# Two lanes of experts, merged third by third, in the mixture-of-experts stage of a two-block kernel

## The chip, the core and the metric

The kernel runs on one core of a Trainium2 chip. The metric is the device time of one execution in microseconds (us); smaller is better. The median of three runs of the kernel before is 2901.98 us (2898.53 to 2902.94).

## What is computed

A first block of two hybrid layers, a second mixer, and then the part that the change touches: a mixture of experts over 512 tokens of width 1024, with 32 experts, 4 chosen for each token, all in float32.

```python
top_vals, top_idx = lax.top_k(logits, TOP_K)
top_gates = jax.nn.softmax(top_vals, axis=-1)
...
gate = xb @ w_gate[e] + b_gate[e]
up = xb @ w_up[e] + b_up[e]
gate = jnp.minimum(gate, SWIGLU_LIMIT)
up = jnp.clip(up, -SWIGLU_LIMIT, SWIGLU_LIMIT)
glu = gate * jax.nn.sigmoid(SWIGLU_ALPHA * gate)
return (glu * (up + 1.0)) @ w_down[e] + b_down[e]
```

Each expert has three 1024 x 1024 float32 matrices, 12 MB, and all 32 are read whatever the routing is: 384 loads of 1 MB.

## The kernel before

The first 1,600 us or so (the dense part) are the two layers and the mixer; the change only moves some of their small constants to another pool. Then `route` and `rank` sort the experts by how many tokens they got. Rank 31 in that order is always expert 0, which is begun before the sorting is done.

**Kinds of expert.** A plan gives each rank its blocks of tokens. In the plan that runs here (`FEW`, line 1928) ranks 0 and 1 have two blocks of 128, ranks 2 to 4 one of 128 and one of 64, ranks 5 to 10 and 31 one of 128, and ranks 11 to 30 one block of at most 64. The text calls them B (0, 1), L (2 to 4), s (5 to 10 and 31) and T (11 to 30). If some expert has more tokens than its blocks hold, another branch runs with the plan `SLOTS`.

**Split and whole weights.** For B, L and s each half of a loaded 1 MB chunk (128 x 1024) is split in two: ACT rounds it to the high part (line 244) and DVE subtracts to get the low part (line 245). The four slots of `ws` hold split halves, and PE multiplies three times (high by high, high by low, low by high). T experts are "twins": PE reads their raw weights as they were loaded (`gu<-raw,xf`, `dn<-raw,hf` in the profile), with no split.

**Thirds.** An expert is three thirds of 4 chunks, 8 halves: gate and up projection for the first half of the features (written here as `r.0`), the same for the second half (`r.1`), and the down projection (`r.2`). Between them `turn` transposes the activations; `find` and `fetch` look up the block's tokens, gather their rows with an indirect DMA, and transpose them.

**Closing.** After a third, its results leave PSUM through ACT and DVE: for a T gate-and-up third ACT's Silu on line 1674 and then DVE; for a T down third two scalings on ACT, line 1747, and a scatter-add by an indirect DMA from POOL; for the others lines 1693, 1766 and their like. `later` collects these instructions, and `catch_up` issues them a few at a time during the third that follows.

**The order.** One list by hand gives the order of ranks: 11, 0, 12, 13, 5, 14, 2, 15, 16, 6, ... (second part of `FEW`). The loop in `ranked` goes gate-and-up 0 of the current rank, down of the rank before, gate-and-up 1 of the current one. So for rank 0 the thirds run 0.0, 11.2, 0.1, 12.0, 0.2, 12.1, 13.0, 12.2, 13.1, 5.0, 13.2, 5.1, ... A third of split weights always follows a T third, 34 times in all after 31.1.

**What sets the order of instructions.** Only PE's are in the order in which the code names them:

```python
with self.tc.manual_schedule(engines={mybir.EngineType.PE}):
```

The instructions of ACT, DVE, POOL and SP are put in order when the program is built, by when the builder reckons that each one's inputs are there. On the chip each engine then runs them in that fixed order.

**Loads.** SP issues all weight loads into a ring of nine 1 MB buffers (`raws`, `NRAW`). A load waits until the chunk nine before it was used: split by ACT and DVE, or, if whole, multiplied by PE. `split_ahead` names loads and splits up to 4 split halves ahead, and up to 12 halves in all.

Of the kernel before, what the change touches and what calls it, by code (L numbers as in the profile page):

```python
# [17 lines left out]
P = 128  # L18
# [26 lines left out]
def _constants():  # L45
# [24 lines left out]
    c[:, C_FEW:C_FEW + NE] = _np.array([sum(s) for s in FEW[0]])[None, :]  # L70
# [135 lines left out]
class _Kernel:  # L206
# [160 lines left out]
    def setup(self):  # L367
# [5 lines left out]
        vecs = self.const.tile([P, NV], F32, name="vecs")  # L373
# [5 lines left out]
        self.ones = self.const.tile([P, P], F32, name="ones")  # L379
        nc.vector.memset(self.ones, 1.0)  # L380
        self.onesr = self.const.tile([P, P], F32R, name="onesr")
        nc.vector.memset(self.onesr.bitcast(F32), 1.0)
        self.identb = self.const.tile([P, P], BF16, name="identb")
        nc.vector.tensor_copy(self.identb, self.ident)
        self.maskb = self.const.tile([P, P], BF16, name="maskb")
# [14 lines left out]
        self.mod = [self.const.tile([P, 48], F32, name="mod%d" % l) for l in range(2)]  # L400

    def position_tables(self):
# [27 lines left out]
        self.sp = self.const.tile([P, 16], F32, name="sp")  # L430
# [6 lines left out]
        self.spr = self.const.tile([P, 16], F32, name="spr")  # L437
        nc.vector.reciprocal(self.spr, self.sp)
        nc.vector.tensor_scalar(self.spr, self.spr, 200.0, 4.0, op0=OP.mult, op1=OP.max)
        self.spn = self.const.tile([P, 16], F32, name="spn")  # L440
        nc.vector.tensor_scalar(self.spn, self.sp, -1.0, None, op0=OP.mult)
        self.hb = self.const.tile([P, 2, 16], F32, name="hb")
# [120 lines left out]
    def slot(self):  # L563
        self.nu += 1
        return self.us[:, self.nu % 4]
# [765 lines left out]
    def rank(self, tp):  # L1331
# [4 lines left out]
        bank = lambda: self.ps2.tile([P, T], F32, tag="gu", name="gu", bufs=4)  # L1336
# [35 lines left out]
        for j in range(4):  # L1372
# [4 lines left out]
                   mo.tile([P, 4, NE], F32, tag="bs", name="gr", bufs=4))  # L1377

        cnt = mo.tile([NE, P], F32R, tag="bs", name="cnt", bufs=4)
# [25 lines left out]
    def down_bias(self, j):  # L1405

        nc = self.nc
        y = self.mo.tile([P, D], F32, tag="yy", name="yb", bufs=3)
        for n in range(2):
            p, w = self.ps2.tile([P, T], F32, tag="dn", name="dn", bufs=2), slice(n * T, (n + 1) * T)  # L1410
# [39 lines left out]
    def overflow(self):  # L1450
# [5 lines left out]
        with tc.For_i(0, n, 1) as it:  # L1456
# [25 lines left out]
            bs = mo.tile([96, P], BF16, tag="bs", name="bs", bufs=4)  # L1482
# [29 lines left out]
    def find(self, b, gate):  # L1512
# [12 lines left out]
        b["idx"] = self.small.tile([P, 1], I32, tag="idx", name="idx", bufs=6)  # L1525
# [7 lines left out]
        b["g"] = self.small.tile([P, 1], F32, tag="gsl", name="gsl", bufs=6)  # L1533
# [47 lines left out]
    def queue(self, srcs):  # L1581

        self.todo += [(s, i, w) for s, w in srcs for i in range(2)]

    def split_ahead(self, n):


        nc = self.nc
        while self.todo and len(self.halves) < 2 * NRAW - 6:
            src, i, whole = self.todo[0]  # L1590
            if not whole and sum(lo is not None for _, lo in self.halves) >= n:
                break
            self.todo.pop(0)
            if i == 0:
                self.raw = self.raws[self.nload % NRAW]
                self.nload += 1
                nc.sync.dma_start(self.raw, src)
            raw = self.raw[:, 1024 * i:1024 * i + 1024]
            if whole:
                self.halves.append((raw, None))  # L1600
                continue
            w = self.ws[self.nsplit % (AHEAD + 1)]
            self.nsplit += 1
            self.split(raw, w[:, 0], w[:, 1])
            self.halves.append((w[:, 0], w[:, 1]))

    def weights(self):
        self.split_ahead(AHEAD + 1)
        self.catch_up(CU + len(self.later) // CV)
        return self.halves.pop(0)  # L1610
# [19 lines left out]
    def gate_up(self, n, bsel, blocks, among=()):  # L1630

        nc, mo = self.nc, self.mo
        among = list(among)
        if blocks[0]["twin"]:
            return self.gate_up_twin(n, bsel, blocks[0], among)
        ps = [[self.ps2.tile([P, T], F32, tag="gu", name="gu", bufs=4) for _ in range(2)] for _ in blocks]
        for c in range(4):
            for i in range(2):
# [9 lines left out]
                self.step(among, k)  # L1648
# [4 lines left out]
    def step(self, among, k):  # L1653
        while among and (among[0][0] <= k or k == KD - 1):
            among.pop(0)[1]()

    def gate_up_twin(self, n, bsel, b, among):


        p = self.ps2.tile([P, T], F32, tag="gu", name="gu", bufs=4)  # L1660
        for k in range(KD):
# [8 lines left out]
            self.step(among, k)  # L1670
# [45 lines left out]
    def down(self, n, blocks):  # L1716
        nc, mo = self.nc, self.mo
        ps = [self.ps2.tile([P, T], F32, tag="dn", name="dn", bufs=2) for _ in blocks]
        for c in range(2):
            for i in range(2):  # L1720
                wt = self.weights()
                for z in range(2):
                    k, w = 2 * i + z, slice(z * T, (z + 1) * T)
                    for p, b in zip(ps, blocks):
                        self.product(p, b, b["h%d" % c], k, [x[:, w] for x in wt], c == 0 and k == 0, c == 1 and k == 3)
        for p, b in zip(ps, blocks):
# [6 lines left out]
    def down_twin(self, b):  # L1733

        nc = self.nc
        p = self.ps2.tile([P, T], F32, tag="dn", name="dn", bufs=2)
        rows = (p[0:64], p[64:P])
        for c in range(2):
            w = [self.weights()[0] for _ in range(4)]
            for k in range(4):  # L1740
                x = slice(k % 2 * T, k % 2 * T + T)
                for z in range(2):
                    self.mm(rows[z], b["h%d" % c][:, k], w[2 * z + k // 2][:, x], c == 0 and k == 0, c == 1 and k == 3)
        b["y"] = y = self.mo.tile([P, D], F32, tag="yy", name="yy", bufs=3)
# [31 lines left out]
    def first_weights(self):  # L1776
        self.todo, self.halves, self.later, self.nsplit, self.nload = [], [], [], 0, 0
# [6 lines left out]
    def experts(self):  # L1784
# [4 lines left out]
        self.us, self.nu, self.nx = mo.tile([P, 4, T], F32, name="u"), 0, 0  # L1789
        self.xts = self.pair(mo, [P, 2, D], "xt")  # L1790
        self.xgs, self.ng = mo.tile([P, XG, D], F32, name="xg"), 0
        nc.gpsimd.memset(self.xgs, 0.0)
        b = self.block(self.pos[:, :, 0], P)
# [13 lines left out]
        state = lambda: (list(self.todo), list(self.halves), self.nsplit, self.nload, self.raw, self.nu, self.nx, self.ng)  # L1807
        kept, first = state(), dict(b)
        with self.tc.If(many == 0) as fits:  # L1809
            self.ranked(cur, *FEW)  # L1810
        with fits.Else():
            self.todo, self.halves, self.nsplit, self.nload, self.raw, self.nu, self.nx, self.ng = kept
            b.clear()
            b.update(first)
            self.ranked(cur, SLOTS, RANKS, True)
            self.overflow()

    def selector(self, r):
        bs = self.mo.tile([96, P], BF16, tag="bs", name="bs", bufs=4)
# [3 lines left out]
    def ranked(self, cur, slots, ranks, more=False):  # L1823

        nc, mo = self.nc, self.mo
        SP = mybir.EngineType.SP
        order = list(self.chosen)

        def blocks_of(r):
            return [self.block(p[:, :, r], n, slots[r] == (64,)) for p, n in zip((self.posS, self.posB), slots[r])]  # L1830

        def start(r, blocks):
            for b in blocks:
                self.find(b, lambda j: self.gates[:, j, r])
            e = nc.values_load(self.order[0:1, r:r + 1], engines=(SP,), min_val=0, max_val=NE - 1)
            order.append(self.chunks(e, slots[r] == (64,)))
            return self.selector(r), blocks

        def down(blocks):
            if blocks[0]["twin"]:  # L1840
                return self.down_twin(blocks[0])
            for n in range(2):
                self.down(n, blocks)


        def tiles(blocks, us):
            c = sum(0.9 if b["twin"] else 1.4 if b["n"] == P else 0.95 for b in blocks)
            return max(0, min(KD - 1, int(us / c)))

        def fetches(cur, nxt, us):  # L1850

            k = tiles(cur, us)
            return [(k + i, f) for i, f in enumerate([f for b in nxt for f in self.fetch(b)])]

        with self.tc.manual_schedule(engines={mybir.EngineType.PE}):
            nxt = start(ranks[0], blocks_of(ranks[0]))
            self.queue(order[1][0])
            self.gate_up(1, *cur, [(0, lambda: self.turn(cur[1], 0))])
            for f in self.fetch(nxt[1][0]):
                f()  # L1860
            for i in range(1, NE):
                prev, cur = cur, nxt
                self.queue(order[i - 1][2:] + order[i][1])
                among = [(tiles(cur[1], 4), lambda: self.turn(prev[1], 1))]
                if i + 1 < NE:
                    r = ranks[i]
                    found, got = blocks_of(r), []
                    among.insert(0, (tiles(cur[1], 2), lambda: got.append(start(r, found))))
                self.gate_up(0, *cur, among)
                if i + 1 < NE:  # L1870
                    nxt = got[0]
                    self.queue(order[i + 1][0])
                else:
                    self.queue(order[i][2:])
                if i == 1 and more:
                    self.overflow_list()
                down(prev[1])
                self.gate_up(1, *cur, [(0, lambda: self.turn(cur[1], 0))] +
                             (fetches(cur[1], nxt[1], 4) if i + 1 < NE else []))
            self.catch_up()  # L1880
            self.turn(cur[1], 1)
            down(cur[1])
            self.catch_up()
# [31 lines left out]
XG = 2  # L1915
# [64 lines left out]
```

## Time and profile before

| | us |
|---|---|
| median of 3 runs | 2901.98 |
| the profiled execution | 2903.9 |
| its span | 2902.0 |
| PE busy, whole span | 2728.3 (94%) |
| experts, from 31.0's first matmul to 30.2's last, about 1683 to 2875 | 1192 |

A profile is one execution. Its span is the time from its first to its last instruction, and 1.9 us lie around it. "Idle before, releaser" says how long an engine stood still before an instruction and what ended that wait. The granted clock of PE is 1.00 at its upper level (2.4 GHz) and 0.50 at its lower one (1.2 GHz); between them a stretch was at both.

### The profile page before, as it was taken

What the parts mean: (1) busy time and instruction counts of PE and PEld (TensorE: products, weight loads), DVE (VectorE), ACT (ScalarE), POOL (GpSimd) and SP (SyncE); (2) the same over time, 40 slices, a digit from 0 to 9 for tenths busy, and PEclk for the clock granted to TensorE, in tenths of its full rate; (3) what the DMA queues carried; (4) which work ended last, traced back from release to release, by engine and by line L of the source; (5) the groups of instructions that cost most, each with busy time, mean ns of one, the idle gap of its engine ahead of it and who ended that gap; (6) DMA issues with size and microseconds to landing.
All of it is one profiled execution on the core that took longest, in us unless ns stands there. A gap on an engine that the chain in (4) does not pass through costs nothing. (4 is left out here: it accounts for less than half of the span.)

```text
span 2902.0 us, 33795 instructions
## 1 busy us (share of the span) xinstructions
PE 2728.3 (94%) x12644; PEld 1927.0 (66%) x12644; DVE 1583.9 (55%) x2601; ACT 1124.0 (39%) x1655; POOL 217.6 (7%) x207
## 2 busy tenths in 40 slices
PE   7989999999999999999999889989999999999985
PEld 5677888888877788888777656546446446446452
DVE  7877676365686663333488664354444345335353
ACT  3644442222554442222344344344333334334342
POOL 0100000000000000000011010110100210110100
PEclk8999999999999999999999989999999999999998
DMA  6332446365221233333221586997997998998995
GB/s 230 122 113 93 160 160 223 118 213 165 94 69 59 65 99 102 95 96 99 89 73 62 190 317 266 338 409 295 384 399 304 346 407 354 366 409 320 371 386 214
DMA packets 126078, 629.42 MB, mean 217 GB/s; under 512 B 15632, under 2 KB 19088, under 8 KB 76752
## 3 DMA queue, kind: packets, MB, share of 16 engines
q1 hardware_dynamic: 111744, 593.94, 54.2%
q0 software_dynamic: 8288, 23.86, 3.8%
q10 hardware_dynamic: 5872, 9.36, 0.9%
q8 instruction: 101, 1.65, 0.2%
q14 instruction: 73, 0.60, 0.1%
HBM read 607.31 MB, written 24.38 MB: 218 GB/s over the span
## 5 line engine op out<-in xcount | busy, mean ns | idle before, releaser
L236 PE MATMUL acc<-hh,whi 128*128 128x512 f32 (+1 forms) x1496 | 574.7, 388 | 13.9 <-ACT hh L506 6.2
L236 PE MATMUL acc<-hh,wlo 128*128 128x512 f32 (+1 forms) x1496 | 576.5, 387 | 5.2 <-DVE wlo L245 5.1
L236 PE MATMUL acc<-hl,whi 128*128 128x512 f32 (+1 forms) x1496 | 574.2, 385 | 0.7 <-DVE hl L507 0.7
L245 DVE TENSOR_TENSOR wlo<-raw,whi 128x1024 fp32r<-128x1024 f32 (+2 forms) x253 | 305.6, 1210 | 268.4 <-ACT whi L244 266.7
L245 DVE TENSOR_TENSOR w<-raw,w 128x1024 fp32r<-128x1024 f32 x288 | 341.1, 1219 | 188.7 <-ACT w L244 186.9
L244 ACT ACTIVATE whi<-raw 128x1024 fp32r<-128x1024 f32 (+2 forms) x253 | 258.9, 1024 | 471.5 <-PE acc L236 417.9
L236 PE MATMUL gu<-w,xth 128*128 128x512 f32 x896 | 313.9, 429 | 44.1 <-ACT w L244 29.0
L244 ACT ACTIVATE w<-raw 128x1024 fp32r<-128x1024 f32 x288 | 293.0, 1051 | 111.6 <-PE gu L236 67.5
L236 PEld LDWEIGHTS acc<-hh,whi 128*128 128x128 f32 x1496 | 282.1, 190 | 78.5 <-ACT hh L506 9.0
L236 PEld LDWEIGHTS acc<-hh,wlo 128*128 128x128 f32 x1496 | 283.3, 189 | 62.4 <-DVE wlo L245 6.3
L236 PEld LDWEIGHTS acc<-hl,whi 128*128 128x128 f32 x1496 | 283.6, 190 | 56.4 <-issue 3.1
L236 PE MATMUL gu<-raw,xf 128*64 128x512 f32 x1280 | 305.8, 601 | 0.7 <-ACT xf L1549 0.7
L236 PEld LDWEIGHTS gu<-w,xth 128*128 128x128 f32 x896 | 173.3, 198 | 100.4 <-ACT w L244 42.7
L236 PE MATMUL gu<-w,xtl 128*128 128x512 f32 x448 | 183.4, 409 | 0.0
L236 PEld LDWEIGHTS gu<-raw,xf 128*64 128x64 f32 x1280 | 82.3, 136 | 128.8 <-issue 122.7
L236 PE MATMUL dn<-w,hTh 128*128 128x512 f32 x448 | 148.0, 407 | 20.5 <-ACT w L244 11.5
L236 PE MATMUL dn<-raw,hf 128*64 128x512 f32 x640 | 143.0, 600 | 0.0
L236 PEld LDWEIGHTS dn<-w,hTh 128*128 128x128 f32 x448 | 85.2, 192 | 56.3 <-ACT w L244 17.6
L1675 DVE TENSOR_SCALAR u<-gu 64x512 f32<-64x512 f32 x40 | 27.3, 682 | 159.7 <-ACT g L1674 159.7
L828 DVE TENSOR_TENSOR t<-t,acc 128x512 f32<-128x512 f32 x44 | 30.3, 688 | 143.6 <-PE acc L236 134.6
L236 PEld LDWEIGHTS dn<-raw,hf 128*64 128x64 f32 x640 | 45.3, 138 | 89.8 <-issue 89.7
L1753 POOL DMA_INDIRECT accd<-yy,idx x37 | 58.3, 1576 | 590.8 <-ACT yy L1766 264.3
(685 smaller groups left out, 3914.8 us busy)
## 6 DMA issues: line engine op xcount, KB each, us to landing
raw<-in_wgu SPq DMA_DIRECT2D x256, 1024.0 KB, 12.5
raw<-in_wd SPq DMA_DIRECT2D x128, 1024.0 KB, 12.3
raw<-in_ws SPq DMA_DIRECT2D x220, 512.0 KB, 3.5
adaw<-in_wada SPq DMA_DIRECT2D x72, 512.0 KB, 4.8
raw<-in_wada SPq DMA_DIRECT2D x24, 512.0 KB, 5.0
raw<-in_ws SPq DMA_DIRECT2D x24, 384.0 KB, 3.0
xy<-in_xT SPq DMA_DIRECT2D x16, 256.0 KB, 4.6
raw<-in_ws SPq DMA_DIRECT2D x9, 256.0 KB
```

The source lines that it names most:

```text
L236: self.nc.tensor.matmul(ps, l, r, start=first, stop=last)
L244: self.nc.scalar.activation(hi, src, AF.Copy)
L245: self.nc.vector.tensor_sub(lo, src, hi.bitcast(F32))
L828: nc.vector.tensor_mul(u, s, ps[1])
L1675: lambda: nc.vector.tensor_scalar(u, p[0:64], 8.0, -6.0, op0=OP.min, op1=OP.max),
L1753: self.nc.gpsimd.indirect_dma_start(out=self.acc_d[:, :], out_offset=bass.IndirectOffsetOnAxis(ap=b["idx"][0:m, 0:1], axis=0), in_=b["y"][ ...
```

## The change

Two lanes are made. One holds rank 31 and then s, B and L experts by turns (31, 5, 0, 6, 1, 7, 2, 8, 3, 9, 4, 10), the other the T experts 11 to 30. `_merged` interleaves their thirds so that each lane's sum of |PE time of a half minus load time of a half| grows alike, by the constants 1.4, 0.95 and 0.9 us of work and 1.3 us of load; a split third is only put behind a T third. The order that comes out begins

```
31.0 31.1 T11.0 31.2 T11.1 5.0 T12.0 5.1 T11.2 5.2 T12.1 0.0 T13.0 0.1 T12.2 T13.1 T14.0 T13.2
0.2 T14.1 T15.0 T14.2 T15.1 6.0 T16.0 6.1 T15.2 6.2 T16.1 1.0 T17.0 1.1 T16.2 T17.1 T18.0 T17.2 1.2
```

and for rank 2 it has `2.0 T 2.1 T T T 2.2`, for ranks 3 and 4 `x.0 T x.1 T T x.2`. `find`, `fetch` and `turn` become jobs with due times on a clock that adds up the constants. Loads are named as soon as the ring has room; splits are named when they are among the next 4 halves, whole ones counted. The PSUM banks of both projections become one pool of six. There is a third gather buffer, for T alone, and `oh` has two buffers, `bs` five, `idx` and `gsl` eight.

```diff
-        vecs = self.const.tile([P, NV], F32, name="vecs")
+        vecs = self.main.tile([P, NV], F32, name="vecs")
...
     def slot(self):
-        self.nu += 1
-        return self.us[:, self.nu % 4]
+        return self.mo.tile([P, T], F32, tag="u", name="u", bufs=4)
...
-        b = {"n": n, "twin": twin, "oh": self.mo.tile([P, 4, P], BF16, tag="oh", name="oh", bufs=3)}
+        b = {"n": n, "twin": twin, "oh": self.mo.tile([P, 4, P], BF16, tag="oh", name="oh", bufs=2)}
...
-        self.ng += 1
-        b["x"] = x = self.xgs[:, self.ng % XG]
+        if not b["twin"]:
+            self.ng += 1
+        b["x"] = x = self.xgs[:, 2 if b["twin"] else self.ng % 2]
...
-        self.todo += [(s, i, w) for s, w in srcs for i in range(2)]
+        self.todo += srcs
+
+    def load_ahead(self):
+
+        while self.todo and self.nload < (self.freed + NRAW if len(self.raws) == NRAW else len(self.raws)):
+            src, whole = self.todo.pop(0)
+            raw = self.raws[self.nload % NRAW]
+            self.nc.sync.dma_start(raw, src)
+            self.loaded += [(raw[:, 1024 * i:1024 * i + 1024], whole, self.nload) for i in range(2)]
+            self.left.append(2)
+            self.nload += 1
...
     def split_ahead(self, n):
...
-        nc = self.nc
-        while self.todo and len(self.halves) < 2 * NRAW - 6:
-            src, i, whole = self.todo[0]
-            if not whole and sum(lo is not None for _, lo in self.halves) >= n:
-                break
...
+        self.load_ahead()
+        while self.loaded and len(self.halves) < n:
+            raw, whole, c = self.loaded.pop(0)
             if whole:
-                self.halves.append((raw, None))
+                self.halves.append((raw, None, c))
                 continue
             w = self.ws[self.nsplit % (AHEAD + 1)]
             self.nsplit += 1
             self.split(raw, w[:, 0], w[:, 1])
-            self.halves.append((w[:, 0], w[:, 1]))
+            self.free(c)
+            self.load_ahead()
+            self.halves.append((w[:, 0], w[:, 1], c))
...
-        ps = [[self.ps2.tile([P, T], F32, tag="gu", name="gu", bufs=4) for _ in range(2)] for _ in blocks]
+        ps = [[self.ps2.tile([P, T], F32, tag="gu", name="gu", bufs=6) for _ in range(2)] for _ in blocks]
...
-                self.step(among, k)
+                self.tick(sum(HALF_US[b["n"], False] for b in blocks))
...
+        def ask(x):
+
+            r = x["r"]
+            x["blocks"] = [self.block(p[:, :, r], n, x["whole"]) for p, n in zip((self.posS, self.posB), plan[r])]
+
+            def find():
+                for b in x["blocks"]:
+                    self.find(b, lambda j: self.gates[:, j, r])
+                x["bs"] = self.selector(r)
+                x["come"] = self.clock + 14.0
+                if x["whole"] or x.get("room"):
+                    fetch(x)
+
+            self.jobs.append((self.clock + 1.5, ("find", r), find))
...
         with self.tc.manual_schedule(engines={mybir.EngineType.PE}):
-            nxt = start(ranks[0], blocks_of(ranks[0]))
-            self.queue(order[1][0])
-            self.gate_up(1, *cur, [(0, lambda: self.turn(cur[1], 0))])
...
+            ask(xs[lanes[1][0]])
+            ask(first["next"])
+            turned(first, 0)
+            for i, (x, p) in enumerate(steps):
+                queue(i)
+                if p == 0:
+                    self.finish_jobs(("find", x["r"]))
...
+                    self.finish_jobs(("fetch", x["r"]))
+                    if x["next"]:
+                        ask(x["next"])
+                if p < 2:
+                    self.gate_up(p, x["bs"], x["blocks"])
+                    turned(x, p)
...
+                self.catch_up()
+                self.finish_jobs(("turn", x["r"]))
+                if x["whole"]:
+                    self.down_twin(x["blocks"][0])
...
+HALF_US = {(128, False): 1.4, (64, False): 0.95, (64, True): 0.9}
+LOAD_US = 1.3
...
+def _merged(plan, lanes):
...
+    one = [(r, p) for r in lanes[0] for p in range(3)]
+    q = lanes[1]
+    two = [(q[0], 0), (q[0], 1)]
+    for a, b in zip(q, q[1:]):
+        two += [(b, 0), (a, 2), (b, 1)]
+    two.append((q[-1], 2))
+    over = lambda r: abs(sum(HALF_US[n, plan[r] == (64,)] for n in plan[r]) - LOAD_US)
+    all1, all2 = sum(over(r) for r, _ in one[2:]), sum(over(r) for r, _ in two)
+    out, one = one[:2], one[2:]
+    d1 = d2 = 0.0
+    while one or two:
+        if one and (not two or d1 / all1 <= 1.1 * d2 / all2 and out[-1][0] in q):
+            out.append(one.pop(0))
+            d1 += over(out[-1][0])
+        else:
+            out.append(two.pop(0))
+            d2 += over(out[-1][0])
+    return out
```

## Rows read from the trace of the kernel before

**Rows 1.** The page, part 1 (PE) and part 2 (granted clock in 40 slices).

```profile
PE 2728.3 (94%) x12644; PEld 1927.0 (66%) x12644; DVE 1583.9 (55%) x2601; ACT 1124.0 (39%) x1655; POOL 217.6 (7%) x207
...
PEclk8999999999999999999999989999999999999998
```

**Rows 2.** Busy time by stretch: length; PE, PEld, DVE, ACT, POOL; clock, DMA share, GB/s.

```profile
1683.00:2875.00 1192.00, 1118.96 (x5105) 627.51 (x5103) 523.29 (x659) 455.08 (x614) 125.70 (x105) 0.97 0.91 353
...
2300.00:2400.00 100.00, 91.91 (x428) 47.17 (x427) 44.60 (x60) 37.62 (x52) 16.48 (x11) 0.97 1.02 410
```

**Rows 3.** Waits from 1690 to 2880: us in total, times, longest.

```profile
PE gu L236 <- ACT w L244: 29.0, 17, 1.9
...
PE gu L236 <- DVE w L245: 15.1, 17, 1.1
...
PE dn L236 <- ACT w L244: 11.5, 7, 1.6
...
PE dn L236 <- DVE w L245: 7.9, 7, 1.1
ACT w L244 <- DMA raw<-in_wgu: 5.9, 2, 3.2
```

**Rows 4.** Groups of instructions, 1690 to 2880: busy, mean ns, idle before.

```profile
L236 PE MATMUL gu<-w,xth 128*128 128x512 f32 x885 | 309.4, 429 | 44.1 <-ACT w L244 29.0 <-DVE w L245 15.1
...
L244 ACT ACTIVATE w<-raw 128x1024 fp32r<-128x1024 f32 x283 | 287.8, 1051 | 108.0 <-PE gu L236 67.5 <-PE dn L236 32.2 <-DMA raw<-in_wgu 5.9
...
L236 PE MATMUL dn<-w,hTh 128*128 128x512 f32 x448 | 148.0, 407 | 20.5 <-ACT w L244 11.5 <-DVE w L245 7.9 <-ACT yy L1766 0.9
```

**Rows 5.** Timeline of ACT behind the T third 16.2: start, length, what.

```profile
2087.67 0.68 ACT L1747 ACTIVATE yy<-dn,gsl 64x512 f32<-64x512 f32 x1 [7.14 <-PE dn L236]
2088.25 1.99 ACT L244 ACTIVATE w<-raw 128x1024 fp32r<-128x1024 f32 x2
2090.27 0.69 ACT L1747 ACTIVATE yy<-dn,gsl 64x512 f32<-64x512 f32 x1
2090.98 2.01 ACT L244 ACTIVATE w<-raw 128x1024 fp32r<-128x1024 f32 x2
```

**Rows 6.** Timeline of PE in the same place.

```profile
2080.51 7.09 PE L236 MATMUL dn<-raw,hf 128*64 128x512 f32 x32
2089.35 0.50 PE L236 MATMUL gu<-w,xth 128*128 128x512 f32 x1 [1.75 <-ACT w L244]
2090.61 0.51 PE L236 MATMUL gu<-w,xth 128*128 128x512 f32 x1 [0.76 <-DVE w L245]
```

**Rows 7.** Timeline of ACT before 0.1 and before 2.1.

```profile
1778.87 3.89 ACT L244 ACTIVATE w<-raw 128x1024 fp32r<-128x1024 f32 x4
1786.11 1.40 ACT L1747 ACTIVATE yy<-dn,gsl 64x512 f32<-64x512 f32 x2 [3.35 <-PE dn L236]
...
1975.05 1.99 ACT L244 ACTIVATE w<-raw 128x1024 fp32r<-128x1024 f32 x2
1980.37 0.69 ACT L1747 ACTIVATE yy<-dn,gsl 64x512 f32<-64x512 f32 x1 [3.34 <-PE dn L236]
1980.96 2.00 ACT L244 ACTIVATE w<-raw 128x1024 fp32r<-128x1024 f32 x2
```

**Rows 8.** By stretch: 2.0, 2.1, 6.1, 1.0, 1.1, four T thirds.

```profile
1947.50:1973.10 25.60, 22.84 (x94) 15.13 (x92) 13.22 (x16) 9.81 (x13) 1.86 (x1) 0.93 0.89 348
1979.90:2002.10 22.20, 22.20 (x102) 15.43 (x100) 8.89 (x9) 9.72 (x13) 2.21 (x2) 1.00 0.93 365
...
2087.20:2104.90 17.70, 15.19 (x64) 10.96 (x62) 10.28 (x9) 10.92 (x13) 2.09 (x2) 0.90 1.02 411
...
2163.70:2194.20 30.50, 27.77 (x114) 20.32 (x112) 14.26 (x18) 10.78 (x15) 1.36 (x1) 0.89 0.90 373
2201.00:2226.10 25.10, 25.10 (x118) 19.37 (x116) 9.96 (x10) 11.30 (x14) 1.71 (x2) 1.00 0.84 321
...
2257.40:2289.70 32.30, 32.30 (x167) 11.38 (x166) 4.56 (x9) 5.98 (x12) 6.29 (x6) 1.00 0.94 332
```

**Rows 9.** Timeline of PE at the first matmul behind the branch.

```profile
1700.54 0.28 PE L236 MATMUL tps<-gates,oh 128*128 128x6 bf16 x4 [3.27 <-DVE oh L1503]
```

**Rows 10.** Timeline of POOL: the clearing of the gather buffers, and what follows.

```profile
1649.71 1.81 POOL L1792 MEMSET xg<- 128x2048 f32 x1 [60.17 <-PE acc L236]
1670.05 0.40 POOL L1317 COPY G<-G 128x256 f32<-128x256 f32 x1 [18.54 <-DVE G L1316]
```

More of the change, by code (lines that the diff above doesn't have):

```diff
@@ L1609, in weights @@
         self.catch_up(CU + len(self.later) // CV)
-        return self.halves.pop(0)
+        hi, lo, c = self.halves.pop(0)
+        self.used.append(c if lo is None else None)
+        if len(self.used) > 4:
+            c = self.used.pop(0)
+            if c is not None:
+                self.free(c)
+        return hi, lo
+    STATE = "todo", "loaded", "halves", "left", "used", "nsplit", "nload", "freed", "nx", "ng"
     def catch_up(self, n=None):
@@ L1651, in gate_up, with gate_up_twin @@
             self.later += self.gated(p, b["n"], b["u%d" % n])
[L1653 to L1660, printed above, removed]
+    def gate_up_twin(self, n, bsel, b):
+        p = self.ps2.tile([P, T], F32, tag="gu", name="gu", bufs=6)
         for k in range(KD):
@@ L1725, in down @@
                         self.product(p, b, b["h%d" % c], k, [x[:, w] for x in wt], c == 0 and k == 0, c == 1 and k == 3)
+                self.tick(sum(HALF_US[b["n"], False] for b in blocks))
         for p, b in zip(ps, blocks):
@@ L1776, in first_weights @@
     def first_weights(self):
-        self.todo, self.halves, self.later, self.nsplit, self.nload = [], [], [], 0, 0
+        self.todo, self.loaded, self.halves, self.left, self.used, self.later = [], [], [], [], [], []
+        self.nsplit, self.nload, self.freed = 0, 0, 0
         self.raws, self.ws = [], []
@@ L1806, in experts @@
         many = nc.values_load(self.many[0:1, 0:1], min_val=0, max_val=1)
-        state = lambda: (list(self.todo), list(self.halves), self.nsplit, self.nload, self.raw, self.nu, self.nx, self.ng)
-        kept, first = state(), dict(b)
+        copied = lambda: {k: list(v) if isinstance(v, list) else v for k, v in ((k, getattr(self, k)) for k in self.STATE)}
+        kept, first = copied(), dict(b)
         with self.tc.If(many == 0) as fits:
-            self.ranked(cur, *FEW)
+            self.ranked(cur, FEW)
@@ L1820, in selector, with ranked @@
         self.nc.gpsimd.tensor_copy(bs, self.perm[:, r:r + 1].bitcast(F32).to_broadcast([96, P]))
         return bs
-    def ranked(self, cur, slots, ranks, more=False):
-        nc, mo = self.nc, self.mo
+    def ranked(self, cur, plan):
         SP = mybir.EngineType.SP
[L1827 to L1853, printed above, removed]
-        with self.tc.manual_schedule(engines={mybir.EngineType.PE}):
-            nxt = start(ranks[0], blocks_of(ranks[0]))
-            self.queue(order[1][0])
-            self.gate_up(1, *cur, [(0, lambda: self.turn(cur[1], 0))])
[L1859 to L1872, printed above, removed]
-                else:
[L1874 to L1879, printed above, removed]
@@ new lines, in ranked @@
+        lanes = _lanes(plan)
+        xs = {r: {"r": r, "whole": plan[r] == (64,)} for lane in lanes for r in lane}
+        for lane in lanes:
+            for r, q in zip(lane, lane[1:] + [None]):
+                xs[r]["next"] = xs.get(q)
+        first = xs[NE - 1]
+        first["bs"], first["blocks"] = cur
+        first["chunks"] = self.chosen[0]
+        steps = [(xs[r], p) for r, p in _merged(plan, lanes)]
+        assert steps.pop(0) == (first, 0)
+        def ask(x):
[9 more added lines that the diff above has]
+            self.jobs.append((self.clock + 1.5, ("find", r), find))
@@ new lines, in fetch, with turned, queue @@
+        def fetch(x):
+            self.jobs += [(x["come"], ("fetch", x["r"]), f) for b in x["blocks"] for f in self.fetch(b)]
+        def turned(x, n):
+            self.jobs.append((self.clock + 3.5, ("turn", x["r"]), lambda: self.turn(x["blocks"], n)))
+        queued = 1
+        def queue(i):
+            nonlocal queued
+            while queued < min(len(steps), i + 4):
+                x, p = steps[queued]
+                if "chunks" not in x:
+                    e = self.nc.values_load(self.order[0:1, x["r"]:x["r"] + 1], engines=(SP,), min_val=0, max_val=NE - 1)
+                    x["chunks"] = self.chunks(e, x["whole"])
+                c = x["chunks"]
+                self.queue(c[p] if p < 2 else c[2:])
+                queued += 1
@@ new lines, in ranked @@
+        with self.tc.manual_schedule(engines={mybir.EngineType.PE}):
+            ask(xs[lanes[1][0]])
[5 more added lines that the diff above has]
+                    self.finish_jobs(("find", x["r"]))
+                    if not x["whole"] and not x.get("room"):
+                        x["room"] = True
+                        fetch(x)
+                    self.finish_jobs(("fetch", x["r"]))
[4 more added lines that the diff above has]
+                    turned(x, p)
+                    y = x["next"]
+                    if p == 1 and y and not x["whole"]:
+                        y["room"] = True
+                        if "come" in y:
+                            fetch(y)
+                    continue
+                self.catch_up()
+                self.finish_jobs(("turn", x["r"]))
+                if x["whole"]:
+                    self.down_twin(x["blocks"][0])
+                else:
+                    for n in range(2):
+                        self.down(n, x["blocks"])
@@ L1880, in ranked @@
             self.catch_up()
-            self.turn(cur[1], 1)
-            down(cur[1])
-            self.catch_up()
+        assert not self.jobs and not self.todo and not self.halves
     def finish_start(self):
@@ L1914 @@
 RAW0 = 5
-XG = 2
 EARLY = 2
```

91 lines of the change are left out of this document (54 added, 37 removed).

## The prediction

> **What bounds the kernel now.** I read the page first, for the engines and TensorE's clock. PE is busy 94% of the span and runs near its upper clock almost throughout [rows 1], so there is little room anywhere. Next I took the stretch of the experts alone, the only one whose order changes: 1192 us, of which PE is busy 1118.96, at a granted clock of 0.97, with the DMA engines busy 0.91 of the time [rows 2]. Both PE and the loads are candidates for the bound, and the change is about balancing the two, so the waits decide. ACT, which splits the chunks, waited only twice and 5.9 us in all for a chunk to land [rows 3]. The weights are 384 chunks of 1.0486 MB, 402.7 MB; in a full stretch they came at 410 GB/s [rows 2], 2.56 us for a chunk and 982 us for all. So the loads have over 150 us to spare, and there is next to no waiting for data that a better balance could remove.
>
> What PE does wait for is the splits: 17 times in gate-up and 7 times in down projections for ACT's high part, and as often for DVE's low part, 29.0 + 15.1 + 11.5 + 7.9 = 63.5 us [rows 3]; the groups give 44.1 + 20.5, with a last 0.9 for a scaling [rows 4]. But those splits were not late for want of data. ACT's idle time before splits is 108.0 us, and nearly all of it ends with PE giving a slot free [rows 4]. A timeline shows what happens. The T third 16.2 ends at about 2087.6; ACT has stood idle 7.14 us in front of that third's first scaling, runs it, then two splits, the second scaling, two splits [rows 5], and PE idles 1.75 and 0.76 us for the first two halves [rows 6]. ACT could have split during the 7.14 us: slots and data were there. It did not, because its order is fixed when the program is built, and there the closing scaling stands ahead of the splits. Before 0.1 it is the other way round: four splits, then the scalings; before 2.1 two splits stand ahead and two behind [rows 7]; in those two places PE waits hardly at all.
>
> So the unit of this kernel is a step from a T third to a split third, and it is **late** where the closing of T comes first on ACT, **early** otherwise. There are 34 such steps, and the counts of the waits say 24 are late (17 + 7 [rows 3]); the ten early ones are x.1 and x.2 of the five large experts.
>
> **What a late step costs.** The idle time is 63.5/24 = 2.65 us. After it PE ran below its upper clock: 2.0, entered late, took 25.6 us at 0.93, 2.1, entered early and equal in work, 22.2 at 1.00; 1.0 late 30.5 at 0.89, 1.1 early 25.1 at 1.00; 6.1 late runs at 0.90 [rows 8]. The differences are 3.4 and 5.4, mean 4.4. The stretch as a whole agrees: clock 0.97 means some 36 us lost in 1192, 1.5 for each late step, and 2.65 + 1.5 = 4.15. I take 4.4, with 3.4 and 5.4 as ends.
>
> **What decides late or early.** The builder puts a split ahead if it reckons that the chunk has come by then. No row shows its reckoned load time, but the four splits before 2.1 bound it: its list puts two ahead of the closing and two behind [rows 7], so in the 22.2 us of 2.0 and the 6.9 of the T third behind it (29 us), 8 chunks but not 9 came, 3.2 to 3.6 us each. I take 3.4, 13.6 us for a third of four chunks, though the real chunk takes 2.56. By that reckoning each third gains or loses lead: B gate-up about 25.1 - 13.6 = +11.5, B down +9, L gate-up +8.6, s about -1, and T 32.3/4 - 13.6 = -5.5 [rows 8]. A step is early if the lead since the ring was last drained is positive. For the kernel before this gives +6 ahead of 0.1 and 1.1, +12 ahead of 0.2 and 1.2, +3.1 ahead of 2.1 and +6.2 ahead of 2.2: all large x.1 and x.2 early, everything else late, as counted.
>
> **The change part by part.** *The order.* x.1 of a large expert still comes one T behind x.0, so it stays early. But 0.2 and 1.2 now come behind four T thirds: 6 + 11.5 - 4 x 5.5 = -4.5, late. 2.2 comes behind three: 3.1 + 8.6 - 16.5 = -4.8, late. 3.2 and 4.2 come behind two: 11.7 - 11 = +0.7, a tie. All s thirds and every x.0 stay late, since at most a single s third or a row of T's stands ahead of them. So 24 late steps become 27 for sure and up to 29; I take 28. Four more at 4.4 is **+17.6 us** (3 x 3.4 = 10 to 5 x 5.4 = 27).
>
> *The start.* PE's first matmul of the lookup waits 3.27 us for DVE behind the branch, ahead of 31.1 [rows 9]. The lookup becomes a job due 1.5 us into 31.1, so that wait goes and other work covers it; the next late thing is the first split of 31.1. I take **-2 us**, between 0 and -3.3.
>
> *The third gather buffer* makes the clearing longer by half, from 1.81 us to an estimated 2.7, on POOL, whose next instruction is 18.5 us later [rows 10]: nothing; without that cover, 0.9.
>
> *Loads and splits.* Loads are named as soon as the ring has room instead of within 12 halves. The ring has nine buffers in both, so SP's wait for the chunk nine before stays; ACT waited 5.9 us for landings, so at most 5.9 is to be gained [rows 3]. Splits still stay at most four ahead, the number of slots.
>
> *PSUM in one pool of six, `oh` with two, `bs` five, `idx` and `gsl` eight, `vecs` and the constants in another pool*: a projection waits for a bank in none of the big groups [rows 4], so more banks give nothing; the third `oh` buffer held a lookup ahead, and the lookups lie a whole third ahead of their use. Nothing for each, and at most one 3.27 us wait like that of rows 9 if the `oh` cover is gone.
>
> *Lookup, gather and turns at due times.* The same instructions on PE, DVE and POOL, and the same gathers on POOL's queue; POOL is busy 125.70 us of 1192 [rows 2], so its queue has room. SP's register loads of the expert's number sit ahead of that expert's chunks as before. Nothing, while PE has thirds of 7 to 25 us to hide them.
>
> The sum is 17.6 - 2 = +15.6 on the profiled execution's 2903.9: 2919.5. That execution lies 1.9 above the median of the runs, so **2918**. The ends are +10 - 3.3 = +7 and +27, so this case's own range is 2909 to 2929.
>
> **The rivals.** *A, faster: the balanced order lets the builder put splits first.* If its reckoned chunk is below some 2.9 us, a pair of T and s thirds no longer loses lead, and early becomes the rule. Half of the 24 late steps gone is -53, **2849**; all gone is -106, 2796. For it: the order is made for just this, with a split third behind a single T wherever it can; the builder's time is inferred from one place. Against it: that place gives 3.2 at least, and by it 384 chunks make 1230 us, over the whole stretch, so that no order could be early on average.
>
> *B, the same: 24 late steps before and after, in other places,* if 3.2, 4.2 and one or two of the T rows tip the other way, or if the late steps in the down projections cost only their idle 2.8 us (19.4/7 [rows 3]). Then the start's -2 is left: **2900**.
>
> *C, faster: the loads set the pace after all.* If naming loads early lifted the mean 353 GB/s to the 410 of the full stretch, PE's busy 1118.96 would be what is left of 1192 [rows 2]: -73, **2829**. Against it stand the two waits of 5.9 us [rows 3]. The Trainium skill ("SBUF — State Buffer", section "Summary: rules for kernel authors") says to reckon with about 358 GB/s between HBM and SBUF. By that rule the loads were at their limit already, and the stage could fall only to 1192 x 353/358 = 1175, an estimate by that page. The 410 of rows 2 speaks against the rule here.
>
> *D, much slower: every step late.* If the new naming of splits (whole halves counted among the next four) puts all 34 behind a closing, it is ten more: 10 x 5.4 = +54, **2956**. Before 0.1 four splits were ahead with the same four slots [rows 7], which speaks against it.
>
> **How the numbers follow.** A measurement tells about 0.2%, 5.8 us, from no change. The forecast has 0.37, D 0.08: slower 0.45. B has 0.17: same 0.17. A has 0.34, C 0.04: faster 0.38. No sign holds most of the chance, so the range takes in A's first half, down to just below 2849, and above it the forecast's end 2929 with part of the way to D: 2845 to 2942. Outside are the full A, C and D, some 0.2.
>
> **What would show it.** If right: about 28 waits of PE for ACT's splits, some 74 us of idle in the two groups of rows 4, a stage of about 1207 us; 0.2, 1.2 and 2.2 begin behind a closing and at a clock below 1.00; 0.1, 1.1, 2.1 stay at 1.00; waits for landed chunks stay small. It is wrong if those waits fall to a few and the stage to 1140 or less (A), if ACT's waits for chunks decide (C), or if PE waits in places that are no step from T to split.

## The result, and the profile after

| | before | changed |
|---|---|---|
| median, us | 2902.06 | 2932.19 (2926.98 to 2935.38) |
| ratio to before | 1 | 1.0104, 95% interval 1.0086 to 1.0123 |
| profiled execution, us | 2903.9 | 2935.38 (span 2933.4) |
| first to last matmul of the experts | 1683 to 2875 | 1706 to 2906 |

The change makes the kernel slower by 30 us, 25 to 36 by the interval. The forecast was 16 slower. In the two profiled executions the stage of the experts, about which the whole forecast was, took 1200 us instead of 1192, and the other 22 us lie ahead of it, in the dense part, which the change touches only by moving some constants to another pool. The 8 us can't be read as the price of the new order: the old stage, with nothing in it changed, took 1192, 1201 and 1199 us in three profiled executions (the kernel before, experiments 2 and 3).

First the stage. The windows view of the changed kernel, which answers to the first line of [rows 2] (length; PE, PEld, DVE, ACT, POOL; clock, DMA share, GB/s):

```profile
1705.00:2906.20 1201.20, 1126.48 (x5101) 628.61 (x5100) 525.09 (x659) 454.63 (x613) 134.45 (x105) 0.96 0.90 349
```

Its waits, which answer to [rows 3]:

```profile
PE gu L236 <- ACT w L244: 31.0, 17, 2.8
PE gu L236 <- DVE w L245: 16.6, 17, 1.1
PE dn L236 <- ACT w L244: 11.9, 7, 1.8
PE dn L236 <- DVE w L245: 7.9, 9, 1.1
PE tps L1540 <- DMA xg<-H,idx: 3.3, 1, 3.3
...
ACT w L244 <- DMA raw<-in_wgu: 2.9, 4, 1.0
```

Again 17 + 7 = 24 late steps, not 28. The gaps in front of the thirds tell which. 0.2, 1.2 and 2.2 have become late (2.5, 2.5 and 2.8 us of idle), 3.2 and 4.2 have stayed early: as worked out, the tie included. But 31.2, 5.2 and 6.2 have become early, which the working had as late. One line of the windows for each of the two kinds, 0.2 and 5.2, from the end of the third ahead:

```profile
1936.50:1962.70 26.20, 23.72 (x105) 18.43 (x104) 9.63 (x8) 11.76 (x14) 1.77 (x1) 1.00 1.01 415
1821.90:1834.50 12.60, 11.96 (x50) 8.78 (x48) 8.56 (x8) 7.98 (x10) 1.47 (x1) 1.00 0.95 350
```

In 0.2 PE is busy 23.72 of 26.20 us; in 5.2 the gap is small. And in 0.2 the clock is 1.00 even behind the late step, as in 1.2 and 2.2, other than in [rows 8]; it stayed at 1.00 in 7 of the 24 thirds entered late and was between 0.82 and 0.94 in the others.

The start did not go as forecast. The 3.27 us wait of [rows 9] is gone and 31.2 is early, but PE now stands still for 3.3 us in front of T11.0, until the rows of the first T expert are gathered (the fifth line of the waits), and T11.0 ran at a clock of 0.79. From 31.0's first matmul to the end of 31.2 it took 56.6 us, and 56.5 before.

Now the dense part. The windows view of the dense matmuls alone (those that write `acc`), up to 1720 us, first of the kernel before, then of the changed one:

```profile
0.00:1720.00 1720.00, 1374.08 (x6060) 1095.99 (x6060) 137.90 (x215) 89.31 (x152) 0.98 0.39 126
```

```profile
0.00:1720.00 1720.00, 1395.77 (x6060) 1093.04 (x6060) 138.30 (x215) 89.25 (x152) 0.98 0.38 122
```

The same 6060 matmuls keep PE busy 21.7 us longer. The engine waits for nothing; it is slower at the same work. In a stretch in which PE never stands still and the clock is 1.00, first before, then after:

```profile
1100.00:1200.00 100.00, 100.00 (x443) 82.81 (x442) 33.78 (x37) 29.44 (x37) 0.00 (x0) 1.00 0.31 95
```

```profile
1100.00:1200.00 100.00, 100.00 (x430) 80.12 (x430) 32.92 (x36) 28.57 (x36) 0.00 (x0) 1.00 0.31 95
```

443 matmuls in 100 us became 430. From start to start, matmuls whose moving operand is `hh` or `hl` took 227.4 ns on average in the trace before (mostly 226 to 228) and 233.3 ns after. Those that move another tile (`a0h` to `a10l`) take 226.7 and 226.8, with the same stationary weights. What differs is where the tiles lie in SBUF. The built programs have these offsets in a partition, in bytes:

```
                         before            changed
hh0                 47808 (64 mod 128)  47616 ( 0 mod 128)
whi (first buffer)  94912 (64 mod 128)  95040 (64 mod 128)
a0h                137920 (64 mod 128) 138048 (64 mod 128)
```

The pools ahead of the dense tiles became 3360 bytes smaller (3488 of constants gone, 128 added by the larger `idx` and `gsl`). Of those constants 3168 bytes now lie ahead of `hh` (192 less in sum) and 320 behind `hl` (128 more for what follows).

### The profile page after: what moved, and what is told of

It is laid out like the page before. It is cut to its first block, busy times and chain, and to the rows that moved or that the text cites. A ratio compares the mean times of both kernels' runs of the same rounds, so it can differ in the third digit from the quotient of the medians.

```text
span 2933.4 us, 33768 instructions
## 1 busy us (share of the span) xinstructions
PE 2757.3 (94%) x12644; PEld 1925.0 (66%) x12644; DVE 1586.4 (54%) x2601; ACT 1125.2 (38%) x1655; POOL 227.6 (8%) x207
## 5 line engine op out<-in xcount | busy, mean ns | idle before, releaser
L236 PE MATMUL acc<-hh,whi 128*128 128x512 f32 (+1 forms) x1496 | 580.7, 392 | 13.7 <-ACT hh L506 6.1
L236 PE MATMUL acc<-hl,whi 128*128 128x512 f32 (+1 forms) x1496 | 580.8, 389 | 1.0 <-DVE hl L507 1.0
L236 PE MATMUL gu<-w,xth 128*128 128x512 f32 x896 | 320.0, 437 | 48.2 <-ACT w L244 31.0
L236 PE MATMUL dn<-raw,hf 128*64 128x512 f32 x640 | 150.7, 604 | 0.0
L236 PEld LDWEIGHTS gu<-w,xtl 128*128 128x128 f32 x448 | 89.6, 200 | 20.0
```

Of the source, the lines that this page charges most:

```text
L236: self.nc.tensor.matmul(ps, l, r, start=first, stop=last)
```

## The experiments

Times are medians on the chip of each run; the kernel before had 2900 to 2901 us beside them.

**1. hh alone moved, in the changed kernel.**

```diff
+        self.sp = self.main.tile([P, 16], F32, name="sp")
         self.hh = [self.main.tile([P, T], F32R, name="hh%d" % k) for k in range(KD)]
...
-        self.sp = self.main.tile([P, 16], F32, name="sp")
```

> The changed kernel with one small tile (sp, 64 bytes a partition) allocated ahead of hh instead of behind hl, so that hh and hl, the moving operands of the dense matmuls, start 64 bytes higher and everything else stays where it is. Theory (the address of the moving operand sets how fast these matmuls follow each other): the interval of saturated acc matmuls on hh and hl falls from 233.3 to 226.7 ns, the experts begin at about 1684 us instead of 1706, and the time is 2932 - 22 = 2910 us; the stage of the experts keeps its 1200 us. Rival (the dense part is slower through the constants that went to another pool, or through the other build order): it stays at 2932.

2912.45 us, ratio 1.0049 (1.003 to 1.0068): 20 us less by the medians, 16 by the ratios. The dense matmuls need 1371.88 us again:

```profile
0.00:1720.00 1720.00, 1371.88 (x6060) 1095.03 (x6060) 138.00 (x215) 89.31 (x152) 0.98 0.39 127
```

**2. hh alone moved, in the kernel before.**

```diff
+        self.pad0 = self.main.tile([P, 16], F32, name="pad0")
         self.hh = [self.main.tile([P, T], F32R, name="hh%d" % k) for k in range(KD)]
         self.hl = [self.main.tile([P, T], F32R, name="hl%d" % k) for k in range(KD)]
+        self.pad1 = self.main.tile([P, 16], F32, name="pad1")
```

> The kernel before with 64 unused bytes in front of hh and 64 behind hl, so that hh and hl start at a multiple of 128 bytes, as in the changed kernel; nothing else of the change is in it. Theory (address): the saturated interval rises from 226.7 to 233.3 ns, the experts begin at about 1705 us, time 2902 + 22 = 2924. Rival (constants in another pool, or the other build order): 2902.

2920.11 us, ratio 1.0069 (1.0052 to 1.0086): 19 slower, by two unused tiles of 64 bytes. The interval on `hh` is 233.2 ns, as the theory has it. The experts began at 1695, not 1705; in one execution that tells little, since in experiment 3, which loses nothing, they began at 1677 and in the kernel before at 1683:

```profile
0.00:1720.00 1720.00, 1389.75 (x6060) 1089.37 (x6060) 138.26 (x215) 89.25 (x152) 0.99 0.38 123
```

**3. hh and all behind it moved together.** As 2, without `pad1`.

> The kernel before with 64 unused bytes in front of hh only, so that everything allocated behind it in the dense part moves up by 64 bytes too: hh, hl, the a tiles (moving operands) and whi, wlo (stationary operands) all start at multiples of 128 bytes, where before all started 64 behind one. The stage of the experts is not moved. Theory 1 (a moving operand at a multiple of 128 bytes is slow by itself): hh, hl and now the a tiles too run at 233.3 ns, time 2901 + 20 + 6 = 2927. Theory 2 (it is slow when moving and stationary operand do not lie alike within 128 bytes): all are alike again, 226.7 ns, time 2901.

2899.78 us, ratio 0.9995 (0.9983 to 1.0007): nothing lost, though all these operands now lie at multiples of 128.

```profile
0.00:1720.00 1720.00, 1370.08 (x6060) 1093.13 (x6060) 137.88 (x215) 89.18 (x152) 0.98 0.39 127
```

So it is not the place of the moving operand by itself; for these matmuls it matters whether moving and stationary operand lie alike within 128 bytes. Theory 1 fell.

**4. The split slots and raw buffers alike,** on top of 1. In the changed kernel two of the four split slots lie at 32 mod 128, as the stationary activations do, and two at 0.

```diff
         self.ws += list(self.wp[z].tile([P, nw, 2, 1024], F32R, name="w").rearrange("p n h c -> n p h c"))
+        if z == 0:
+            self.pad2 = self.wp[0].tile([P, 24], F32, name="pad2")
```

> The changed kernel with hh and hl 64 bytes higher, and with 96 unused bytes behind the first part of the weight ring, so that all four split slots and all raw buffers of the experts start 32 bytes behind a multiple of 128, as the stationary activations do. Theory (moving and stationary operand must lie alike within 128 bytes): the saturated interval of the two slots that lay at a multiple of 128 falls from 233.5 to 228 ns; half of the 2000 matmuls on split weights by 5 ns is 5 us, more if the T thirds, whose raw weights move too, gain as well: 2912 - 5 = 2907 or below. Rival (only the dense matmuls mind, since the experts wait elsewhere): 2912.

2905.59 us, ratio 1.002 (1.0011 to 1.0029): 7 less than in 1. Intervals below 240 ns on split weights have a mean of 228.5 ns instead of 231.3; in the kernel before it was 229.9. That is 2.8 ns for each of 2304 matmuls, 6.4 us. The group of gate-up on the high part of the activations, in 1 and in 4:

```profile
L236 PE MATMUL gu<-w,xth 128*128 128x512 f32 x857 | 307.0, 437 | 47.6 <-ACT w L244 31.0 <-DVE w L245 16.6
```

```profile
L236 PE MATMUL gu<-w,xth 128*128 128x512 f32 x860 | 302.2, 430 | 47.6 <-ACT w L244 30.9 <-DVE w L245 16.7
```

**5. The old order in the changed kernel.** The merged list is replaced by the old one, and the lane of the larger experts put in its order; all else is as changed, the slow `hh` included.

```diff
-        steps = [(xs[r], p) for r, p in _merged(plan, lanes)]
+        steps = [(xs[r], p) for r, p in (_listed() if plan is FEW else _merged(plan, lanes))]
```

> The changed kernel with the thirds in the order of the kernel before; jobs, loads, banks, buffers and addresses as changed. Theory (the stage's 9 us come from the addresses of two of the four slots and from small things, not from the order, since the late steps are 24 in both): late steps 24, with 0.2, 1.2 and 2.2 early again and 31.2, 5.2 and 6.2 late again, stage about 1200, time 2930. Rival (the order itself costs the 9 us, by the steps in front of the large experts): stage 1191, time 2923. If my count before the result was the whole story (each late step more costs 4.4 us), time moves by 4.4 for each late step that the two differ by.

2918.55 us, ratio 1.0063 (1.0046 to 1.008), 12 to 14 less than the changed kernel. My theory of no difference fell: by the medians the order costs. The waits:

```profile
PE gu L236 <- ACT w L244: 30.8, 16, 3.0
PE gu L236 <- DVE w L245: 14.3, 16, 1.1
PE dn L236 <- ACT w L244: 9.8, 6, 1.6
PE dn L236 <- DVE w L245: 6.8, 6, 1.1
```

22 late steps, since 31.2 and 0.0 are early with the new jobs and loads. The merged order has two more, but that is not where the profiles show the 12 to 14 us. 0.0, 0.2, 1.2 and 2.2, late only with the merged order, took 12.3 us more with it, and 5.2 and 6.2, late only with the old one, 8.6 us less: 3.7 together. Another 10 us lie in the 20 thirds that are entered late with both, at nearly the same idle time but a lower clock. The kernel before and experiment 2, with one and the same stage, differ by 9.6 us in just this way. So by what the order costs stays open.

**6. ACT, too, in the order of the code,** in the changed kernel.

```diff
-        with self.tc.manual_schedule(engines={mybir.EngineType.PE}):
+        with self.tc.manual_schedule(engines={mybir.EngineType.PE, mybir.EngineType.Activation}):
```

> The changed kernel with ACT, too, kept in the order in which the code names its instructions, in the stage of the experts. Theory (late steps are made by the builder's order on ACT): splits stand ahead of the closing of a T third, PE's waits for ACT's and DVE's splits fall from 24 and 24 to a few, the clock of the stage rises to 0.99, and up to 24 x 4.2 = 100 us go: about 2835. Rival (the data would not have been there, or closings and turns get late behind waiting splits): new waits of PE for turns and banks, the time 2932 or above.

2888.68 us, ratio 0.9963 (0.9948 to 0.9977): 43 less (the theory had up to 100), and faster than the kernel before in spite of the slow `hh`. ACT's timeline in front of 6.1, in the changed kernel and in this one:

```profile
2020.89 0.59 ACT L1699 ACTIVATE g<-gu 64x512 f32<-64x512 f32 x1 [3.00 <-PE gu L236]
2021.39 3.88 ACT L244 ACTIVATE w<-raw 128x1024 fp32r<-128x1024 f32 x4
```

```profile
2003.77 3.89 ACT L244 ACTIVATE w<-raw 128x1024 fp32r<-128x1024 f32 x4
2007.69 0.59 ACT L1699 ACTIVATE g<-gu 64x512 f32<-64x512 f32 x1
```

The four splits now stand ahead of the Silu that closes 16.0. What is late next is the Silu itself, and PE, which runs into a turn of activations that are not there:

```profile
PE tps L1729 <- DVE u L1701: 22.7, 13, 4.4
PE tps L1729 <- DVE u L1719: 9.8, 5, 3.2
PE gu L236 <- ACT w L244: 6.4, 3, 2.9
PE gu L236 <- DVE w L245: 2.9, 5, 0.9
```

**7. Edits 1 and 6 together.**

> The changed kernel with hh and hl 64 bytes higher and with ACT, too, in the order of the code. Theory (address and late steps are independent): 20 us less than with ACT's order alone, 2868. Rival (the dense part and the stage share a limit): more than 2875.

2868.00 us, ratio 0.9878 (0.986 to 0.9895). The two are independent.

**8. The old order on top of 7.**

> The same with the thirds in the order of the kernel before. Theory (the merged order costs its 14 us only by the steps that it makes late, and no step is late when ACT goes by the code): within 4 us of the run with the merged order, 2868. Rival (the merged order has a price of its own, by loads, turns or banks): 14 us less, 2854. Second rival (the merged order does even out loads, which shows only now): slower than 2868, by waits for chunks to land.

2882.77 us, ratio 0.9934 (0.9917 to 0.995): now the old order is the slower one, by 15 us, so my theory fell and the second rival held. PE's waits for ACT's splits rose from 6.3 to 14.1 us. ACT's waits for landed chunks, with the merged and with the old order:

```profile
ACT w L244 <- DMA raw<-in_wgu: 21.7, 12, 6.7
ACT w L244 <- DMA raw<-in_wd: 7.7, 6, 2.3
```

```profile
ACT w L244 <- DMA raw<-in_wgu: 60.0, 23, 6.8
ACT w L244 <- DMA raw<-in_wd: 3.8, 4, 1.9
```

**9. Edit 6 in the kernel before.**

> The kernel before with ACT, too, in the order in which the code names its instructions, in the stage of the experts. Theory (late steps are the builder's order on ACT): the 24 waits for splits fall to a few, up to 24 x 4.4 = 105 us less, of which new waits for late turns take some half as in the changed kernel: about 2855. Rival (the splits here are named up to 12 halves ahead, so ACT waits in front of closings for chunks that have not landed): waits of ACT for raw over 30 us, little gain, 2890 or above.

2915.73 us, ratio 1.0044 (1.0028 to 1.0061): slower by 15. The rival held. No step is late any more, as in the theory, but here splits are named further ahead, so ACT stands in front of chunks that are still to come, with the closings behind them:

```profile
ACT w L244 <- DMA raw<-in_wgu: 125.1, 27, 15.1
...
ACT w L244 <- DMA raw<-in_wd: 19.7, 11, 3.7
```

```profile
PE tps L1540 <- ACT hf L1707: 54.3, 8, 8.6
PE tps L1704 <- DVE u L1694: 29.8, 10, 4.7
```

**10. Later turns on top of 7.**

```diff
-            self.jobs.append((self.clock + 3.5, ("turn", x["r"]), lambda: self.turn(x["blocks"], n)))
+            self.jobs.append((self.clock + 8.0, ("turn", x["r"]), lambda: self.turn(x["blocks"], n)))
```

> The kernel with hh moved and ACT in the order of the code, with the turn of an expert's activations due 8 us after its third instead of 3.5. Theory (splits ahead of closings make the closings late, and PE runs into the turn too early: 18 waits, 33.3 us): these waits fall below 10 us, time 2868 - 20 = 2848. Rival (the turn is then late for the down projection or the next third): waits of PE for hTh or hf instead, 2865 or above.

2828.05 us, ratio 0.9748 (0.9733 to 0.9763): 40 less, twice the 20 that was expected; the waits for late turns fell from 33.3 to 2.2 us. Of the changed kernel's 24 waits for ACT's splits 4 are left (3 in experiment 7), and of 18 for late turns one:

```profile
PE gu L236 <- ACT w L244: 6.0, 3, 2.8
...
PE dn L236 <- ACT w L244: 1.0, 1, 1.0
PE tps L1729 <- DVE u L1701: 2.2, 1, 2.2
```

From experiment 1 to here 20 late steps went and 84 us with them: 4.2 us for each, as a mean over all that went with them (the T thirds, too, became 11.5 us shorter in sum).

**11. All together** (1, 4, 6 and 10).

> All three together: hh, slots, ACT in the order of the code, turns due after 8 us. If the gains add: 2848 - 5 = 2843, about 2% below the kernel before. If the loads become the bound: more waits of ACT and PE for chunks to land (now 29 us on ACT), 2848 or above.

2821.90 us, ratio 0.9731 (0.9717 to 0.9746), 78 us below the kernel before and 21 below what was expected.

```profile
1685.00:2792.60 1107.60, 1084.36 (x5100) 614.64 (x5100) 522.00 (x659) 455.60 (x612) 126.15 (x105) 0.99 0.97 378
```

The stage takes 1108 us, PE is busy for 1084 of them, and the DMA engines are at 0.97.

**12. The old order on top of 11.**

> The fastest kernel so far (hh, slots, ACT in the order of the code, turns due after 8 us) with the thirds in the order of the kernel before. Theory (the merged order evens out the loads, and that is worth something once splits stand ahead of closings): ACT waits for chunks to land clearly longer than the 100 us of the merged order, PE gets some of it, 2822 + 15 = 2837. Rival (the 15 us between the two orders came from turns that came too early): within 4 us of 2822.

2856.38 us, ratio 0.985 (0.9825 to 0.9874): 34 us slower, more than expected. ACT's waits for chunks differ little (100.2 us with the merged order, 113.3 with the old one), but with the old order more of it reaches PE, here in 9 waits for gate-up splits instead of 2 and in 7 for chunks of the down projection instead of 4. With the merged order, then with the old one:

```profile
PE gu L236 <- ACT w L244: 5.7, 2, 2.9
PE gu L236 <- DVE w L245: 4.0, 8, 0.8
PE dn L236 <- DMA raw<-in_wd: 3.3, 4, 1.3
```

```profile
PE gu L236 <- ACT w L244: 16.4, 9, 2.9
PE gu L236 <- DVE w L245: 9.9, 14, 0.9
PE dn L236 <- DMA raw<-in_wd: 8.2, 7, 1.7
```

## Why the prediction came out as it did

The sign was right, but that the time fell into the range is luck. This case's own range, 2909 to 2929, missed it by 3 us, the part above that was left for rival D, which did not come, and most of the 30 us came from an edit that I had costed at nothing. With the address effects out (experiment 4) the changed kernel is only 3 to 8 us slower than the kernel before (some 3 more if its slots were as in that kernel); that is what became of the 15.6 us of the sum.

- **The late step as the unit of the stage: right in kind.** With ACT in the order of the code and later turns, 20 of them and 84 us went (experiments 1 and 10), 4.2 us for each as a mean, against the forecast's 4.4. Of a single one this says less: the six steps that changed between the two orders (experiment 5) were worth 2.3 to 4.6 us each.
- **"24 late steps become 28": mis-sized.** The changed kernel has 24, and 22 with the old order and all else changed, so the order adds two, not four. 0.2, 1.2 and 2.2 came out late and 3.2 and 4.2 early, but 5.2 and 6.2 early too: my ledger gave every T third the same -5.5, while the one ahead of 5.2 has the turns and takes 10.7 us, not 8.1. That this is the reason is not shown, and 7.2, 8.2 and 9.2 are late behind T thirds of 10.0 to 10.2 us. The builder's load time of 3.4 us, from which the ledger was made, is argued only.
- **The order's +17.6: measured 12 to 14** (the changed kernel against experiment 5). By what it costs them stays open, as said there.
- **The start's -2: measured nothing.** The wait for the lookup went, but one of 3.3 us for the first T expert's gather came in its place. "Nothing, while PE has thirds of 7 to 25 us to hide them" fails here: the lookup that is due later makes the gather later. It was issued 5 us before 31.1 ended, and in the kernel before 11 us.
- **"`vecs` and the constants in another pool [...] Nothing for each": the step that failed.** It cost 16 to 20 us (experiments 1 to 3). I asked which instruction would wait, and none does; the same instructions became longer, because tiles that the change never names were moved by 192 and 128 bytes. The same effect lies in the slots (7 us, experiment 4), some 3 of them new with the change: 231.2 against 229.9 ns over the 2304 matmuls on split weights.
- **Jobs, loads and splits, "nothing": about right.** Experiment 5 less these 16 to 20 and 3 leaves 0 to 5 us below the kernel before, by subtraction only. In its profile 0.0, now early, takes 24.1 us instead of 29.1.
- **Rival A: did not come.** The late steps stayed 24. The balanced order was worth something only with the builder's order of ACT out of the way: 15 us with ACT in the order of the code (7 against 8), and 34 when turns come later (11 against 12). That is another mechanism than A's, and only in 8 do ACT's waits for chunks show it clearly. Its bound of 2.9 us for a chunk goes by an s third of some 15 us; by the ledger's s third, 12.6 us, it would have been 2.6.
- **Rival B: its count came true,** 24 late steps before and after, in other places. With the address effects out the time, 2905.6, lies nearer to its 2900 than to 2918.
- **Rival C: not the bound here** (ACT waited 2.9 us for chunks of gate-up), but near it in experiment 11, where the whole stage moved 378 GB/s. The Trainium skill's figure of about 358 GB/s ("SBUF — State Buffer", section "Summary: rules for kernel authors") is no ceiling in this case.

## What to carry to other kernels

When a change moves tiles between pools, compare the addresses of the operands of the hottest instructions before and after, whether or not the change names them; a matmul's time from start to start in a stretch that never idles shows it at once. An order made to balance engines can act only if the instructions it wants early are not fixed behind others on their own engine: look at the order on the engine that feeds the bound first. And when one wait is removed, look for the next one that it uncovers; here the later turns gave as much again as the splits had. And the time of a stage in one profile is not yet the time of the stage: here it moved by 9 us with nothing changed in it, so small prices are read from medians of several executions.

## What the runs showed of the hardware

A 128x512 matmul in a saturated stretch at the upper clock took 226.7 to 227.4 ns from start to start where the moving and the stationary operand lay alike within 128 bytes (both at 64, both at 0), and 233.3 ns where the moving one lay at 0 and the stationary one at 64, 2.6 to 2.9% more, with PE shown as busy throughout. In the experts of the changed kernel, gate-up on split weights took 229.2 ns with 32 and 32 and 233.8 with 0 and 32. But in the kernel before, where slots at 0 and at 64 met activations at 64, the means were 230.2 and 230.1: no difference. So the rule is not complete, and other distances were not tried; whether 128 bytes is the true period is open.

The Trainium skill ("TensorE: Matmul & The Clock Gate", section "Step-by-step: what each phase is for") says that the moving operand and the weight load have read ports of their own, so that loading the next weights takes no bandwidth from the running matmul. The measured intervals don't fit that without an exception: experiments 2 and 3 differ in where the stationary operand lies, 64 bytes, and in little else that these matmuls read, and the matmuls on `hh` took 233.2 ns and 227.3 ns from start to start. So the place of the one matters to the rate of the other; what the two reads share is not shown.
